# Hybrid decoder trunk on one core: in the last two feed-forward layers the high weights meet both activation parts in one 512-column product

## The chip, the cores and the metric

The kernel runs on one core of one Trainium2 chip. The metric is the device time of one execution in microseconds; of several runs the median counts. The engines are named as in the profile: PE is TensorE (PEld its weight loads), DVE is VectorE, ACT is ScalarE, POOL is GpSimd, SP issues most of the DMAs.

## The reference

The input is a sequence of 256 tokens with 1024 features, float32. Four residual layers follow one another; each applies a token mixer (attention, gated spatial unit, state-space layer, attention again) and then a channel mixer, the feed-forward block that the change is about:

```
def causal_depthwise_conv(h, w, b):
    hp = jnp.pad(h, ((0, 0), (CONV_K - 1, 0), (0, 0)))
    y = hp[:, 0:L] * w[0]
    for kk in range(1, CONV_K):
        y = y + hp[:, kk:kk + L] * w[kk]
    return y + b

def conv_gated_ffn(xn, w_up, conv_w, conv_b, w_down):
    h = causal_depthwise_conv(xn @ w_up, conv_w, conv_b)   # 1024 -> 2 * 2816
    a, g = jnp.split(h, 2, axis=-1)
    return (jax.nn.silu(g) * a) @ w_down                   # 2816 -> 1024

for i in range(4):
    x = x + mixer_i(rmsnorm(x, ...))
    x = x + conv_gated_ffn(rmsnorm(x, ...), ...)
return rmsnorm(x, final_norm_g)
```

## The kernel before, in words

**Split products.** Every matrix product keeps float32 precision by splitting both factors into a high part (rounded to the matmul's input format fp32r) and a low part (the rest). A product is then three matmuls into the same PSUM region: high weights by high activations, high weights by low activations, low weights by high activations. `mm_feat` (lines 119 to 126) does this with the weights as the stationary operand and the activations as the moving one: line 124 is wh by xth, line 125 is wh by xtl, line 126 is wl by xth, each with 256 columns, the 256 tokens. `mm_tok` (lines 128 to 134) does it the other way round, with 256 or 512 columns of weights as the moving operand. The activations lie in two tiles, `xth` and `xtl` of [128, 8, 256], made by `new_xt` and filled by `xt_evac`.

**Weights.** `Weights` streams tiles of 1 MB through three raw buffers. `half` turns half a tile into its high part on ACT (line 71) and its low part on DVE (line 72); there are six buffers for each part. Each iteration of a loop prepares one tile, four tiles ahead of use: two halves are called from `evac` (lines 414 and 418), the rest from `step`.

**Phases.** The plan runs eight phases one after the other: attention, feed-forward 0, gated unit, feed-forward 1, state-space layer (S5), feed-forward 2, attention, feed-forward 3. The program fixes the order of instructions on each engine; engines wait for one another by semaphores.

**The feed-forward phase.** There are 22 "up" units, u0 to u21. Each has two blocks of 128 output features: s=1, the gate, and s=0, the value. There are 11 "down" units, d0 to d10. `proj_feat` does one s of one up unit: 8 steps of k, each three matmuls, so 24 matmuls for an s and 48 for a unit. `down` does 24 matmuls of 512 columns. PSUM has eight banks of 512 float32: banks 0 to 3 hold the sums of the down products; u_m writes bank 4 + m%4, s=0 in the left half, s=1 in the right half. u0, u1 and u2 are done early, in the heads of the phase, token by token, and are transposed (line 368) into banks 4, 5 and 6 in the middle of u3, which itself writes bank 7. The order is then u4, u5, d0, u6, u7, d1, and so on to u16, u17, d6, then u18, u19, u20, u21, d7, and the tail d8, d9, d10, once for each half of the tokens.

**Evacuation.** `evac` of a unit stands in program order behind the matmuls of the next unit. For each s, ACT reads the bank and writes y = tap 2 times the value plus bias (line 406); then DVE adds the other two taps from the same bank, shifted by one and two tokens (line 410, two instructions for each s, so four a unit). Then come half a weight tile, silu on ACT (line 416), the gate product on DVE (line 417), another half a tile, and the split of the result into gh (ACT) and gl (DVE), lines 198 and 199. In the iteration of u3, `evac` handles u0, u1 and u2 together; u3's own `evac` comes in the iteration of u4. The loop also calls `w.step()` after each `evac`.

**S5** uses the space of the `xth` and `xtl` tiles for two tables, TT, once their last products are done (lines 1114 to 1121).

Of the kernel before, what the change touches and what calls it, by code (L numbers as in the profile page):

```python
# [8 lines left out]
F32 = mybir.dt.float32  # L9
F32R = mybir.dt.float32r  # L10
BF16 = mybir.dt.bfloat16
AF = mybir.ActivationFunctionType
ALU = mybir.AluOpType
# [84 lines left out]
class K:  # L98
# [65 lines left out]
        return r  # L164

    def new_xt(self):
        self.xth = self.big.tile([128, 8, 256], F32R, tag="xth", name="xth")
        self.xtl = self.big.tile([128, 8, 256], F32R, tag="xtl", name="xtl")

    def to_xt(self, b, xn, banks):  # L170
        for q in range(2):
# [38 lines left out]
    def proj_feat(self, n, p, s):  # L210

        for k in range(8):
            self.mm_feat(p[:, 256 * s:256 * s + 256], n, slice(256 * k + 128 * s, 256 * k + 128 * s + 128),
                         k, s == 0 and k == 0, s == 1 and k == 7)

    def proj_tok(self, n, b, p):

        t = slice(128 * b, 128 * b + 128)
        for k in range(8):
            self.mm_tok(p, self.xth[:, k, t], self.xtl[:, k, t], n, slice(256 * k, 256 * k + 256), k == 0, k == 7)  # L220
# [106 lines left out]
class FFN(Phase):  # L327
# [44 lines left out]
    def body(self):  # L372
        k, w = self.k, self.k.w
        pend = []
        for kind, a in self.order()[3:-3]:
            n = w.take()
            if kind == "u":
                p = k.bank(4 + a % 4)
                k.proj_feat(n, p, 0)
                if a == 3:  # L380
                    for m in range(3):
                        self.transposes(m, k.bank(4 + m))
                        pend.append((m, k.bank(4 + m)))
                k.proj_feat(n, p, 1)
                e = [(a, p)]
            else:
                k.down(self.gt[a], n, self.acc, (0, 1), a == 0, False)
                e = []
            self.evac(pend)
            pend = e  # L390
            w.step()
            for _ in range(1 + (kind == "d" and a % 2)):
                next(self.bg, None)
        self.evac(pend)
        for _ in self.bg:
            pass

    def evac(self, items):
        nc, cw = self.nc, self.cw
        ys = []  # L400
        for m, p in items:
            y = self.tmp.tile([128, 512], F32, tag="y", name="y")
            ys.append(y)
            for s in (1, 0):
                cs = slice(256 * s, 256 * s + 256)
                nc.scalar.activation(y[:, cs], p[:, cs], AF.Identity, scale=cw[:, s, m, 2:3], bias=cw[:, s, m, 3:4])  # L406
            for s in (1, 0):
                o = 256 * s
                for tap in (1, 2):
                    nc.vector.scalar_tensor_tensor(  # L410
                        y[:, o + tap:o + 256], p[:, o:o + 256 - tap], cw[:, s, m, 2 - tap:3 - tap],
                        y[:, o + tap:o + 256], ALU.mult, ALU.add)
        w = self.k.w
        w.half_to(w.use + w.ap)
        for (m, p), y in zip(items, ys):
            nc.scalar.activation(y[:, 256:512], y[:, 256:512], AF.Silu)  # L416
            nc.vector.tensor_tensor(out=y[:, 0:256], in0=y[:, 256:512], in1=y[:, 0:256], op=ALU.mult)  # L417
        w.half_to(w.use + w.ap)
        for (m, p), y in zip(items, ys):
            if m % 2 == 0:  # L420
                self.gt[m // 2] = self.k.new_gt()
            self.k.split(self.gt[m // 2], m % 2, y[:, 0:256])
# [313 lines left out]
class S5(Phase):  # L736
# [368 lines left out]
    def body(self):  # L1105
        k, nc, w = self.k, self.nc, self.k.w
        ut = k.pst[:, 4:8, :].rearrange("p b (a t) -> p (b a) t", a=2)
        n = w.take()
# [2 lines left out]
            FFN.transposes(self, m, k.bank(4 + m))  # L1111
        k.proj_feat(n, k.bank(7), 1)
        tabs = [w.take() for _ in range(5)]
        TT = []
        for i, tag in enumerate(("xth", "xtl")):
            t = k.big.tile([128, 2048], F32, tag=tag, name=f"T{i}")
            TT.append(t)

        for c in (slice(0, 512), slice(512, 1536)):
            for i in range(2):  # L1120
                nc.sync.dma_start(TT[i][:, c], self.d_t[i][:, c.start + 512:c.stop + 512])
        gt0, p0, bb, gt1, p1 = (w.hl[t] for t in tabs)
# [21 lines left out]
        def scan(i, mid=lambda: None):  # L1144
# [10 lines left out]
            sh = [128, 2, 8, 64]  # L1155
            T = [self.t0[:, 512 * r:512 * r + 512] if i == 0 else TT[r][:, 512 * (i - 1):512 * i] for r in range(2)]
            T = [v.rearrange("p (a c) -> p a c", a=8).unsqueeze(1).to_broadcast(sh) for v in T]
# [107 lines left out]
        n = w.take()  # L1265
# [113 lines left out]
```

## Time and profile before

| | |
|---|---|
| median of 3 runs | 1209.46 us (1208.31 to 1211.32) |
| the profiled execution, its own time | 1211.12 us |
| its span, first to last instruction | 1209.3 us |
| mean granted TensorE clock | 0.990 |
| matmuls, weight loads | 9072 each |
| DVE busy | 895.8 us (74%) |
| ACT busy | 707.3 us (58%) |

A row of the timeline gives the start in us, the length in us, engine, line, operation, output and inputs with shapes, and the count of merged instructions; a bracket at its end gives the idle time before it and what ended it. A row of instruction groups gives the count, then busy time in us and the mean of one in ns, then the idle time before the group. Matmuls are pipelined: the length printed for one overlaps with the next, so the pace of PE is read from the distance between starts. A row of the stages gives, for each engine, busy us and the number of instructions, and at the end the granted TensorE clock (1.00 is full), the DMA share and GB/s.

### The profile page before, as it was taken

How to read it: one execution, taken by the hardware profiler on the slowest of the kernel's cores; microseconds unless marked ns; L12 is line 12 of the kernel's file. 1: busy time of each engine (PE TensorE's matmuls, PEld its weight loads, DVE VectorE, ACT ScalarE, POOL GpSimd, SP SyncE). 2: the span in 40 equal slices, each digit the busy share in tenths (PEclk: the TensorE clock that was granted, in tenths of full speed). 3: DMA queues.
4: the chain of work that ended last, by engine and by line, in shares of the span. 5: the costliest groups of instructions: out<-in, count | busy, mean ns of one | idle time of the engine just before them, and what ended most of it. 6: DMA issues, size and time to landing. Idle time of an engine off the chain costs nothing.

```text
span 1209.3 us, 21995 instructions
## 1 busy us (share of the span) xinstructions
PE 1182.2 (98%) x9072; PEld 1083.6 (90%) x9072; DVE 895.8 (74%) x1268; ACT 707.3 (58%) x1076; POOL 166.3 (14%) x308
## 2 busy tenths in 40 slices
PE   8999999999999999999987999999999999999997
PEld 6898999999898999999976899999988989999996
DVE  5665689799767599899569769776766656886673
ACT  5665576557554574667474657565555655665551
POOL 3885000000286001000122000000000000000000
PEclk8999999999999999999998999999999999999999
DMA  7633368787656355777861645645535333564530
GB/s 295 224 105 122 144 220 283 232 296 258 233 209 209 114 218 220 228 268 263 316 251 68 224 180 194 243 161 202 193 120 225 109 123 112 207 242 175 209 123 35
DMA packets 49557, 237.46 MB, mean 196 GB/s; under 512 B 14896, under 2 KB 15792, under 8 KB 24240
## 3 DMA queue, kind: packets, MB, share of 16 engines
q1 hardware_dynamic: 46208, 223.73, 51.3%
q0 software_dynamic: 3104, 12.06, 2.5%
q8 instruction: 71, 1.16, 0.4%
q10 hardware_dynamic: 144, 0.26, 0.1%
q14 instruction: 30, 0.25, 0.1%
HBM read 222.79 MB, written 13.24 MB: 195 GB/s over the span
## 4 chain that ended last, share of the span: by engine, by line
PE 90%; DVE 5%; ACT 2%; DMA 1%; issue 1%; DVEq 0%; SPq 0%; POOLq 0%; POOL 0%; ACTq 0%
PE pst L124 15%; PE pst L126 15%; PE pst L125 15%; PE pst L132 13%; PE pst L134 13%; PE pst L133 13%; PE pst L536 1%; PE pst L179 1%; DVE wl L72 1%; PE pst L512 1%; DVE t L1166 1%; PE pst L553 1%; DVE wl L68 1%; DVE t L1169 1%; ACT wh L71 1%
## 5 line engine op out<-in xcount | busy, mean ns | idle before, releaser
L72 DVE TENSOR_TENSOR wl<-raw,wh 128x1024 fp32r<-128x1024 f32 x344 | 415.0, 1231 | 60.0 <-ACT wh L71 59.8
L124 PE MATMUL pst<-xth,wh 128*128 128x256 f32 x1552 | 441.0, 284 | 0.0
L125 PE MATMUL pst<-xtl,wh 128*128 128x256 f32 x1552 | 439.2, 283 | 0.0
L126 PE MATMUL pst<-xth,wl 128*128 128x256 f32 x1552 | 439.1, 283 | 0.0
L71 ACT ACTIVATE wh<-raw 128x1024 fp32r<-128x1024 f32 x344 | 350.3, 1048 | 9.4 <-DMA raw<-in_up_dram 4.3
L124 PEld LDWEIGHTS pst<-xth,wh 128*128 128x128 f32 x1552 | 297.7, 192 | 2.3
L125 PEld LDWEIGHTS pst<-xtl,wh 128*128 128x128 f32 x1552 | 297.8, 192 | 1.2
L126 PEld LDWEIGHTS pst<-xth,wl 128*128 128x128 f32 x1552 | 297.7, 192 | 0.0
L410 DVE SCALAR_TENSOR_TENSOR y<-pst,cw,y 128x255 f32<-128x255 f32 x352 | 160.7, 479 | 72.8 <-ACT y L406 66.6
L132 PE MATMUL pst<-wh,gh 128*128 128x512 f32 x512 | 202.7, 396 | 1.6 <-ACT gh L689 1.6
L133 PE MATMUL pst<-wl,gh 128*128 128x512 f32 x512 | 201.0, 393 | 0.0
L134 PE MATMUL pst<-wh,gl 128*128 128x512 f32 x512 | 200.8, 392 | 0.0
L406 ACT ACTIVATE y<-pst,cw 128x256 f32<-128x256 f32 x176 | 88.1, 557 | 69.4 <-PE pst L126 64.9
L132 PEld LDWEIGHTS pst<-wh,gh 128*128 128x128 f32 x512 | 97.1, 190 | 21.7 <-ACT gh L689 2.1
L134 PEld LDWEIGHTS pst<-wh,gl 128*128 128x128 f32 x512 | 96.8, 189 | 21.1 <-DVE gl L690 0.4
L133 PEld LDWEIGHTS pst<-wl,gh 128*128 128x128 f32 x512 | 97.0, 190 | 18.6
L132 PE MATMUL pst<-wh,xth 128*128 128x256 f32 (+1 forms) x336 | 105.9, 315 | 0.0
L134 PE MATMUL pst<-wh,xtl 128*128 128x256 f32 (+1 forms) x336 | 105.3, 313 | 0.0
L133 PE MATMUL pst<-wl,xth 128*128 128x256 f32 (+1 forms) x336 | 105.3, 313 | 0.0
L163 POOL TENSOR_TENSOR r<-m,mhalf 128x1 f32<-128x1 f32 x20 | 11.1, 554 | 684.7 <-DVE m L161 676.2
L416 ACT ACTIVATE y<-y 128x256 f32<-128x256 f32 x88 | 36.4, 419 | 75.3 <-DVE y L410 75.3
L198 ACT ACTIVATE gh<-y 128x256 fp32r<-128x256 f32 x88 | 36.1, 418 | 75.2 <-DVE y L417 75.2
(167 smaller groups left out, 1219.2 us busy)
## 6 DMA issues: line engine op xcount, KB each, us to landing
raw<-in_up_dram SPq DMA_DIRECT2D x88, 1024.0 KB, 5.0
raw<-in_down_dram SPq DMA_DIRECT2D x44, 1024.0 KB, 4.9
raw<-in_wqk_dram SPq DMA_DIRECT2D x16, 1024.0 KB, 4.9
raw<-in_wo_dram SPq DMA_DIRECT2D x8, 1024.0 KB, 4.8
raw<-in_glu_dram SPq DMA_DIRECT2D x8, 1024.0 KB, 5.9
raw<-in_wv_dram SPq DMA_DIRECT2D x7, 1024.0 KB, 5.2
gb<-in_g_dram SPq DMA_DIRECT2D x9, 512.0 KB, 5.7
d_gt<-gf POOLq DMA_DIRECT2D x4, 1024.0 KB, 7.7
```

The source lines that it names most:

```text
L71: nc.scalar.activation(h[:, s], r[:, s], AF.Copy)
L72: nc.vector.tensor_tensor(out=l[:, s], in0=r[:, s], in1=h[:, s], op=ALU.subtract)
L124: nc.tensor.matmul(out, h[:, cols], xh, start=first, stop=False, skip_group_check=True)
L125: nc.tensor.matmul(out, h[:, cols], xl, start=False, stop=False, skip_group_check=True)
L126: nc.tensor.matmul(out, l[:, cols], xh, start=False, stop=last, skip_group_check=True)
L132: nc.tensor.matmul(out, ah, h[:, cols], start=first, stop=False, skip_group_check=True)
L133: nc.tensor.matmul(out, ah, l[:, cols], start=False, stop=False, skip_group_check=True)
L134: nc.tensor.matmul(out, al, h[:, cols], start=False, stop=last, skip_group_check=True)
L198: self.nc.scalar.activation(g[0][:, j], src, AF.Copy)
L406: nc.scalar.activation(y[:, cs], p[:, cs], AF.Identity, scale=cw[:, s, m, 2:3], bias=cw[:, s, m, 3:4])
L410: nc.vector.scalar_tensor_tensor(y[:, o + tap:o + 256], p[:, o:o + 256 - tap], cw[:, s, m, 2 - tap:3 - tap], y[:, o + tap:o + 256], ALU.mu ...
L416: nc.scalar.activation(y[:, 256:512], y[:, 256:512], AF.Silu)
```

## The change

In feed-forward 2 and 3 (`self.i > 1`), the units u4 to u21 use a new function, `proj_wide`. The two activation parts lie side by side for each k in one tile `xt` of [128, 8, 2, 256]; the names `xth` and `xtl` become views of it, and S5's two tables become halves of one tile in its place. For each k, the high weights are loaded once and meet both parts in one matmul of 512 columns: the left half of the bank gets wh by xth, the right half wh by xtl. A second matmul of 256 columns adds wl by xth to the left half. A unit now fills two banks, s=0 one and s=1 the next: 4 and 5 for even units, 6 and 7 for odd ones. `evac` first copies both right halves to a tile z on ACT, then DVE adds the left halves to it in place; from there it goes on as before, but reads z (SBUF) where it read the bank (PSUM). The rest of the kernel is the same, u0 to u3 and feed-forward 0 and 1 included.

```
     def new_xt(self):
-        self.xth = self.big.tile([128, 8, 256], F32R, tag="xth", name="xth")
-        self.xtl = self.big.tile([128, 8, 256], F32R, tag="xtl", name="xtl")
+        self.xt = self.big.tile([128, 8, 2, 256], F32R, tag="xt", name="xt")
+        self.xth, self.xtl = self.xt[:, :, 0], self.xt[:, :, 1]
...
+    def proj_wide(self, n, p):
+        h, l = self.w.hl[n]
+        for s in range(2):
+            for k in range(8):
+                c = slice(256 * k + 128 * s, 256 * k + 128 * s + 128)
+                self.nc.tensor.matmul(p[:, s], h[:, c], self.xt[:, k].rearrange("p a t -> p (a t)"),
+                                      start=k == 0, stop=False, skip_group_check=True)
+                self.nc.tensor.matmul(p[:, s, 0:256], l[:, c], self.xth[:, k], start=False, stop=k == 7,
+                                      skip_group_check=True)
...
         for kind, a in self.order()[3:-3]:
             n = w.take()
-            if kind == "u":
+            if kind == "u" and a > 3 and self.i > 1:
+                p = k.pst[:, 4 + 2 * (a % 2):6 + 2 * (a % 2)]
+                k.proj_wide(n, p)
+                e = [(a, p)]
+            elif kind == "u":
                 p = k.bank(4 + a % 4)
...
         for m, p in items:
+            if len(p.shape) == 3:
+                z = self.tmp.tile([128, 2, 256], F32, tag="z", name="z")
+                nc.scalar.activation(z[:, :, :], p[:, :, 256:512], AF.Copy)
+                nc.vector.tensor_tensor(out=z[:, :, :], in0=p[:, :, 0:256], in1=z[:, :, :], op=ALU.add)
+                p = z[:, :, :].rearrange("p s t -> p (s t)")
             y = self.tmp.tile([128, 512], F32, tag="y", name="y")
...
-        TT = []
-        for i, tag in enumerate(("xth", "xtl")):
-            t = k.big.tile([128, 2048], F32, tag=tag, name=f"T{i}")
-            TT.append(t)
+        t = k.big.tile([128, 2, 2048], F32, tag="xt", name="T")
+        TT = [t[:, i] for i in range(2)]
```

## The prediction

> **What bounds the kernel now.** I read the profile's page first, then the chain of waits, the instruction groups, and the timeline of feed-forward 2. The page's first rows and the chain agree on the bound:
>
> ```profile
> PE 1182.2 (98%) x9072; PEld 1083.6 (90%) x9072; DVE 895.8 (74%) x1268; ACT 707.3 (58%) x1076; POOL 166.3 (14%) x308
> PE 90%; DVE 5%; ACT 2%; DMA 1%; issue 1%; DVEq 0%; SPq 0%; POOLq 0%; POOL 0%; ACTq 0%
> ```
>
> PE is the chain for 90% of the span. So an edit pays if it shortens PE's stream, and costs if it makes PE wait. How long a matmul really occupies PE stands in the distance between starts, here at the end of an up unit, at the down unit behind it, and at another down unit:
>
> ```profile
> 805.75 0.28 PE L124 MATMUL pst<-xth,wh 128*128 128x256 f32 x1
> 808.51 0.28 PE L126 MATMUL pst<-xth,wl 128*128 128x256 f32 x1
> 808.63 0.40 PE L132 MATMUL pst<-wh,gh 128*128 128x512 f32 x1
> 812.29 0.39 PE L133 MATMUL pst<-wl,gh 128*128 128x512 f32 x1
> 760.22 0.39 PE L134 MATMUL pst<-wh,gl 128*128 128x512 f32 x1
> 762.93 0.39 PE L134 MATMUL pst<-wh,gl 128*128 128x512 f32 x1
> 787.15 1.91 DVE L410 SCALAR_TENSOR_TENSOR y<-pst,cw,y 128x255 f32<-128x255 f32 x4 [4.05 <-ACT y L406]
> 804.13 1.91 DVE L410 SCALAR_TENSOR_TENSOR y<-pst,cw,y 128x255 f32<-128x255 f32 x4 [4.05 <-ACT y L406]
> ```
>
> From 805.75 to 808.51 there are 23 steps: 0.120 us for 256 columns. From 808.63 to 812.29 there are 16 steps of 512 columns, 0.2288 us each; from 760.22 to 762.93 there are 12, 0.2258 each. For whole units I use the period of one group (two up units, one down unit): the same evacuation recurs 16.98 us later; 96 matmuls at 0.120 are 11.52, which leaves 5.46 for 24 matmuls, 0.2275 each. Twice 256 columns cost 0.240 us, once 512 costs 0.2275. Something of about 13 ns is paid per matmul.
>
> **The change, part by part.** *The wide product.* Each step of k and s had three narrow matmuls, 0.360 us. It now has one wide and one narrow, 0.2275 + 0.120 = 0.3475: 12.5 ns less (11.2 to 14.2 by the two other rows). Units u4 to u21 have 18 x 16 = 288 such steps a layer, so 3.6 us a layer, 7.2 in both, if PE never waits. The count of columns through the array is the same; only 576 matmuls with their weight loads are gone.
>
> *The banks.* A unit now takes two banks, and u5's s=1 takes bank 7. Before, u5 had bank 5 and bank 7 was next written by u7. Bank 7 holds u3, which is evacuated the old way, behind the evacuations of u0, u1 and u2. This is how DVE and PE stood at that place:
>
> ```profile
> 726.75 5.54 DVE L410 SCALAR_TENSOR_TENSOR y<-pst,cw,y 128x255 f32<-128x255 f32 x12 [0.70 <-ACT y L406]
> 732.21 1.21 DVE L72 TENSOR_TENSOR wl<-raw,wh 128x1024 fp32r<-128x1024 f32 x1
> 733.34 1.08 DVE L417 TENSOR_TENSOR y<-y 128x256 f32<-128x256 f32 x3
> 734.35 1.22 DVE L72 TENSOR_TENSOR wl<-raw,wh 128x1024 fp32r<-128x1024 f32 x1
> 735.48 1.09 DVE L199 TENSOR_TENSOR gl<-y,gh 128x256 fp32r<-128x256 f32 x3
> 736.49 2.35 DVE L72 TENSOR_TENSOR wl<-raw,wh 128x1024 fp32r<-128x1024 f32 x2
> 738.76 1.90 DVE L410 SCALAR_TENSOR_TENSOR y<-pst,cw,y 128x255 f32<-128x255 f32 x4
> 743.52 1.91 DVE L410 SCALAR_TENSOR_TENSOR y<-pst,cw,y 128x255 f32<-128x255 f32 x4
> 726.68 0.28 PE L124 MATMUL pst<-xth,wh 128*128 128x256 f32 x1
> 737.83 0.28 PE L124 MATMUL pst<-xth,wh 128*128 128x256 f32 x1
> 1046.83 0.28 PE L124 MATMUL pst<-xth,wh 128*128 128x256 f32 x1
> 1047.76 1.90 DVE L410 SCALAR_TENSOR_TENSOR y<-pst,cw,y 128x255 f32<-128x255 f32 x4
> ```
>
> DVE has no gap here from 726.75 on. The row at 738.76 is u3's four taps; they end at 738.76 + 1.90 = 740.66, and only then is bank 7 free. On PE, 726.68 is the second step of u3's s=1. Seven steps of 0.36 end u3 at 729.20, the 16 of u4 lead to 734.96 and eight of u5's s=0 to 737.83, where u5's s=1 began. With wide products PE gets there 24 x 0.0125 = 0.3 us earlier, at 737.53. Nothing on DVE or ACT ahead of 740.66 is changed, so PE stands until DVE is done. How soon PE follows the engine it waits for:
>
> ```profile
> 384.96 0.64 ACT gh L689
> 385.64 0.50 PE L132 MATMUL pst<-wh,gh 128*128 128x512 f32 x1 [1.63 <-ACT gh L689]
> 386.36 0.70 PE L134 MATMUL pst<-wh,gl 128*128 128x512 f32 x1
> 390.12 0.40 PE L134 MATMUL pst<-wh,gl 128*128 128x512 f32 x1
> 384.00:385.00 1.00, 0.00 (x1) 0.00 (x0) 0.89 (x2) 0.04 (x1) 0.00 (x0) 1.00 0.91 320
> 387.00:388.00 1.00, 1.00 (x4) 0.81 (x3) 1.00 (x2) 0.48 (x1) 0.00 (x0) 0.50 0.96 352
> 390.00:391.00 1.00, 1.00 (x6) 0.81 (x5) 0.45 (x1) 0.29 (x2) 0.00 (x0) 1.00 0.54 123
> ```
>
> ACT ended at 385.60, PE started at 385.64: 0.04 us. So u5's s=1 starts at 740.70 and not at 737.83: 2.87 us late, after a wait of 740.70 - 737.53 = 3.17 us. In feed-forward 3 the taps end at 1049.66 and the old start was 1046.83: 2.87 again. Queued behind the waiting matmul on PE is all that follows: the rest of u5, d0, u6. On the other side u4's s=1 needs bank 5 some 2.8 us after 729.20; the second third of the 12 taps, u1's, ends 3.7 us after 726.75, at 730.4. It does not wait. u5's s=0 needs bank 6 at 734.7, free at 732.3.
>
> Behind that point 264 steps are left in the layer (8 of u5, 16 units of 16): 264 x 0.0125 = 3.30 us are won back (2.96 to 3.75). What was won ahead of it is swallowed by the wait.
>
> *The clock.* The rows above show what a stop of PE does besides. PE stood for 1.63 us by the bracket (the row of 384 to 385 has nothing of PE busy) and from 386.36 ran at half clock (0.50 in the row of 387 to 388) until about 390. From 386.36 to 390.12 there are 9 steps of 512 columns in 3.76 us, where 9 x 0.2275 is 2.05: 1.71 us lost. The new wait is longer, so I expect the same drop in both layers. There it came 2.35 us after PE stopped (386.36 less 384.01); in a wait of 3.17 some 0.8 us of the slow stretch could fall into the wait itself, which lowers the loss to 1.71 x 2.94 / 3.76 = 1.3. I take 1.6 (1.3 to 1.7).
>
> *Copy and sum.* The work that evacuation gains, by its nearest rows:
>
> ```profile
> L406 ACT ACTIVATE y<-pst,cw 128x256 f32<-128x256 f32 x176 | 88.1, 557 | 69.4 <-PE pst L126 64.9
> L198 ACT ACTIVATE gh<-y 128x256 fp32r<-128x256 f32 x88 | 36.1, 418 | 75.2 <-DVE y L417 75.2
> L185 ACT ACTIVATE xth<-pst 128x512 fp32r<-128x512 f32 x32 | 17.7, 596 | 35.8 <-PE pst L179 35.7
> L190 DVE TENSOR_TENSOR x<-pst,x 128x512 f32<-128x512 f32 x28 | 19.1, 688 | 23.7 <-PE pst L134 23.7
> 809.89 1.91 DVE L410 SCALAR_TENSOR_TENSOR y<-pst,cw,y 128x255 f32<-128x255 f32 x4 [0.91 <-ACT y L406]
> 872.35 1.91 DVE L410 SCALAR_TENSOR_TENSOR y<-pst,cw,y 128x255 f32<-128x255 f32 x4 [0.91 <-ACT y L406]
> 877.17 2.36 DVE L72 TENSOR_TENSOR wl<-raw,wh 128x1024 fp32r<-128x1024 f32 x2
> 883.56 0.69 DVE L190 TENSOR_TENSOR x<-pst,x 128x512 f32<-128x512 f32 x1 [4.03 <-PE pst L134]
> ```
>
> ACT copies 512 elements from PSUM in 0.60 us (L185), DVE adds 512 in 0.69 (L190). y then comes from SBUF, 0.42 instead of 0.56 (L198 for L406). The taps can begin 0.60 + 0.69 + 0.42 - 0.56 = 1.15 us later. In a group DVE idles 4.05 + 0.91 = 4.96 us ahead of its two evacuations; the group gets 0.4 us shorter and the two evacuations 2.3 longer, so 2.2 us of idle are left. Weights are prepared four tiles ahead, over 16 us of PE. This costs nothing as long as that idle lasts. u18 to u21 have no down unit between them: there only 0.91 is free for each against 1.15 + 0.2, and DVE falls back by 4 x 0.44 = 1.8 us. Behind u21, gl was done at 877.17, and d10 needed it: the first sum over d10 came at 883.56, behind its first 6 matmuls, so d10 began near 882.2. Of 5.0 us, 1.8 + 1.15 are used; about 2 remain. Banks come free earlier than before, with the add.
>
> *One tile for both parts, and T in its place.* The same engines read and write the same elements in the same order; the two old tiles were released by matmuls standing next to each other. Nothing, at most one matmul (0.12 us) either way.
>
> *The sum.* Per layer 2.87 + 1.6 - 3.30 = +1.2 us (0.8 to 3.2 for both layers from the bounds), together +2.3. The profiled execution took 1211.12 us for a span of 1209.3, so it would be 1213.4; against the median of 1209.46, 1.7 below that execution, it is 1211.8. That is 0.2% slower, inside the 0.3% (3.6 us) that a measurement of this kernel can tell from no change.
>
> **The rivals.** *No wait at bank 7*, if PE does not in fact reach it ahead of DVE: then the full 7.2 us come in, 1202.3. Against it stands DVE's row without a gap to 740.66; u3 would have to be evacuated over 3 us earlier. 8%.
>
> *The wait without the clock drop*: 2 x (2.87 - 3.30) = -0.9 us, 1208.6. The Trainium skill speaks for it: "TensorE: Matmul & The Clock Gate", section "What's actually happening", lets the clock fall to half only after an idle window of about 3.4 us, longer than this wait. The trace does not agree: 1.63 us idle were followed by a clock of 0.50. 14%.
>
> *The wide product saves nothing*, because a 512-column matmul with activations as the moving operand takes as long as two narrow ones. Then the late start and the slow clock stay and nothing is won back: 2 x (2.87 + 1.6) = +8.9 us, 1218.4. This is the slower case; it goes over +3.6 us once a step saves less than (4.47 - 1.8) / 264 = 10 ns. For it: no row of before streams 512 columns of activations. Against it:
>
> ```profile
> L132 PE MATMUL pst<-wh,xth 128*128 128x256 f32 x240 | 68.3, 284 | 0.0
> L124 PE MATMUL pst<-xth,wh 128*128 128x256 f32 x1552 | 441.0, 284 | 0.0
> ```
>
> At 256 columns it makes no difference which of the two streams, 284 ns each. The same page of the Trainium skill, section "Back-to-back issue gap", points the same way as this rival: columns / 2.4 + 2.5 ns make a pair only 2.5 ns dearer than one wide product; by it, as an estimate, the sum would be about +7.6 us. The trace has 12.5. 6%.
>
> *DVE becomes the bound* in u18 to u21 or the tail, if copy and sum cost twice what I took. That is beyond any row here: 2%.
>
> **How the numbers follow.** The forecast has 70%: 1210.3 to 1212.7 by its bounds, and medians scatter by about 1.5 us. With the case without a clock drop (1208.6, or 1207.7 with the larger saving) the range is 1206 to 1215. Left out are the other cases and some tails. Faster by over 0.3% (below 1205.8): the first rival and a little, 0.10. Slower (above 1213.1): the last two, 8%, and the upper end of the forecast, 12%: 0.20. Within: 0.70.
>
> **What would show it.** Right: in both layers one gap of PE of about 3.2 us in the middle of u5, ended by DVE's taps of u3; behind it a granted clock of 0.5 for over 3 us; wide and narrow starts 0.2275 and 0.120 apart; no other gap on PE. Wrong: no gap there, a second gap at u20 or d10, or a step of 0.36.

## The result, and the profile after

The changed kernel is slower: 1216.61 us median of 6 runs (1215.24 to 1220.81) against 1209.94 (1208.31 to 1211.46) for the kernel before, a ratio of 1.0058 with a 95% interval of 1.0041 to 1.0076. The profiled execution took 1216.67 us, its span is 1214.9 us, 5.6 us more than before. The forecast was 1211.8 with a range of 1206 to 1215.

The page shows the removed matmuls, and that the chain is still PE's: 576 matmuls fewer, and yet hardly less busy time.

```profile
PE 1180.1 (97%) x8496; PEld 1053.7 (87%) x8496; DVE 919.5 (76%) x1304; ACT 725.7 (60%) x1112; POOL 166.1 (14%) x308
PE 89%; DVE 6%; ACT 2%; issue 1%; DMA 1%; DVEq 0%; SPq 0%; POOLq 0%; ACTq 0%
```

In the changed kernel's numbering, line 223 is the wide product, 225 the narrow one, 420 the copy to z, 421 the sum, 427 the tap with the bias, 431 the two other taps. The waits of PE from feed-forward 2 to the end are these (line, releaser: us in all, times, longest):

```profile
PE pst L223 <- DVE y L431: 5.9, 2, 3.0
PE pst L557 <- DVE sl L548: 0.5, 1, 0.5
```

The second stood in the kernel before as well. The first is new: one wait of 3 us in each of the two layers, ended by DVE's taps. Here is the place in feed-forward 2: on DVE the twelve taps of u0 to u2 and u3's four, then on PE the last narrow product ahead of the wait, the first wide product of u5's second half, and the first matmul of the down unit behind it:

```profile
726.48 5.54 DVE L431 SCALAR_TENSOR_TENSOR y<-pst,cw,y 128x255 f32<-128x255 f32 x12 [0.70 <-ACT y L427]
738.49 1.90 DVE L431 SCALAR_TENSOR_TENSOR y<-pst,cw,y 128x255 f32<-128x255 f32 x4
737.29 0.28 PE L225 MATMUL pst<-xt,wl 128*128 128x256 f32 x1
740.54 0.47 PE L223 MATMUL pst<-xt,wh 128*128 128x512 f32 x1 [2.97 <-DVE y L431]
744.89 0.47 PE L132 MATMUL pst<-wh,gh 128*128 128x512 f32 x1
```

The granted clock is the number third from the right in these rows of the stages:

```profile
738.00:739.00 1.00, 0.00 (x0) 0.00 (x0) 0.96 (x2) 0.35 (x1) 0.00 (x0) 1.00 1.03 434
743.00:744.00 1.00, 1.00 (x4) 0.84 (x4) 0.93 (x2) 0.03 (x1) 0.00 (x0) 0.50 0.16 25
```

The taps end at 740.39, PE goes on at 740.54. The eight steps of that half take from 740.54 to 744.89, 4.35 us, at a granted clock of 0.50 in the row of 743 to 744.

The pace of the products, in an undisturbed unit and the down unit behind it:

```profile
806.44 0.40 PE L223 MATMUL pst<-xt,wh 128*128 128x512 f32 x1
806.67 0.28 PE L225 MATMUL pst<-xt,wl 128*128 128x256 f32 x1
811.74 0.40 PE L223 MATMUL pst<-xt,wh 128*128 128x512 f32 x1
811.97 0.28 PE L225 MATMUL pst<-xt,wl 128*128 128x256 f32 x1
812.09 0.40 PE L132 MATMUL pst<-wh,gh 128*128 128x512 f32 x1
817.59 0.39 PE L223 MATMUL pst<-xt,wh 128*128 128x512 f32 x1
```

From 806.44 to 812.09 there are 16 steps of a wide and a narrow product: 0.353 us each. It was 0.360 with three narrow ones; the prediction had 0.3475. A step saves 7.0 ns instead of 12.5.

With these sizes the prediction's own sum comes out. The start at bank 7 stands 740.54 + 0.27 - 737.83 = 2.98 us late (DVE's row of twelve taps, here at 726.48, stood at 726.75 before, so 0.27 puts the two traces on one scale). The slow clock costs 4.35 - 8 x 0.353 = 1.53 us. Won back are 264 x 7.0 ns = 1.85 us. That makes 2.7 us a layer and 5.3 for both; the spans differ by 5.6, and 5.9 from this place on, where the changed kernel is 0.27 ahead. Most of the rest lies in the down units, which the prediction took as unchanged. Behind an alternating unit one takes 5.50 us (812.09 to 817.59 above); before, it took 5.47, from 808.63 to the first matmul of the next up unit:

```profile
814.10 0.28 PE L124 MATMUL pst<-xth,wh 128*128 128x256 f32 x1
```

There are fourteen such down units in the two layers, which makes 0.4 to 0.5 us.

### The profile page after: what moved, and what is told of

Same layout as the page of the kernel before. It is cut to its first block, busy times and chain, and to the rows that moved or that the text cites. A ratio compares the mean times of both kernels' runs of the same rounds, so it can differ in the third digit from the quotient of the medians.

```text
span 1214.9 us, 20913 instructions
## 1 busy us (share of the span) xinstructions
PE 1180.1 (97%) x8496; PEld 1053.7 (87%) x8496; DVE 919.5 (76%) x1304; ACT 725.7 (60%) x1112; POOL 166.1 (14%) x308
## 4 chain that ended last, share of the span: by engine, by line
PE 89%; DVE 6%; ACT 2%; issue 1%; DMA 1%; DVEq 0%; SPq 0%; POOLq 0%; ACTq 0%
PE pst L132 13%; PE pst L134 13%; PE pst L133 13%; PE pst L223 10%; PE pst L124 9%; PE pst L125 9%; PE pst L126 9%; PE pst L225 5%; PE pst L557 1%; PE pst L179 1%; DVE wl L72 1%; PE pst L533 1%; DVE t L1185 1%; PE pst L574 1%; DVE y L431 1%
## 5 line engine op out<-in xcount | busy, mean ns | idle before, releaser
L124 PE MATMUL pst<-xt,wh 128*128 128x256 f32 x976 | 278.1, 285 | 0.0
L125 PE MATMUL pst<-xt,wh 128*128 128x256 f32 x976 | 276.1, 283 | 0.0
L126 PE MATMUL pst<-xt,wl 128*128 128x256 f32 x976 | 276.1, 283 | 0.0
L223 PE MATMUL pst<-xt,wh 128*128 128x512 f32 x576 | 207.0, 403 | 5.9 <-DVE y L431 5.9
L124 PEld LDWEIGHTS pst<-xt,wh 128*128 128x128 f32 x976 | 187.2, 192 | 1.7
L125 PEld LDWEIGHTS pst<-xt,wh 128*128 128x128 f32 x976 | 187.2, 192 | 0.7
L126 PEld LDWEIGHTS pst<-xt,wl 128*128 128x128 f32 x976 | 187.2, 192 | 0.0
L225 PE MATMUL pst<-xt,wl 128*128 128x256 f32 x576 | 163.0, 283 | 0.0
L223 PEld LDWEIGHTS pst<-xt,wh 128*128 128x128 f32 x576 | 109.6, 190 | 33.6 <-ACT y L437 6.5
L225 PEld LDWEIGHTS pst<-xt,wl 128*128 128x128 f32 x576 | 110.2, 191 | 0.5
L132 PE MATMUL pst<-wh,xt 128*128 128x256 f32 (+1 forms) x336 | 105.9, 315 | 0.0
L134 PE MATMUL pst<-wh,xt 128*128 128x256 f32 (+1 forms) x336 | 105.3, 313 | 0.0
L133 PE MATMUL pst<-wl,xt 128*128 128x256 f32 (+1 forms) x336 | 105.2, 313 | 0.0
```

The costliest lines, as they stand in the source:

```text
L124: nc.tensor.matmul(out, h[:, cols], xh, start=first, stop=False, skip_group_check=True)
L125: nc.tensor.matmul(out, h[:, cols], xl, start=False, stop=False, skip_group_check=True)
L126: nc.tensor.matmul(out, l[:, cols], xh, start=False, stop=last, skip_group_check=True)
L132: nc.tensor.matmul(out, ah, h[:, cols], start=first, stop=False, skip_group_check=True)
L133: nc.tensor.matmul(out, ah, l[:, cols], start=False, stop=False, skip_group_check=True)
L134: nc.tensor.matmul(out, al, h[:, cols], start=False, stop=last, skip_group_check=True)
```

## Experiments

The question left by the two traces: are the wait and the slow clock the whole loss, and why does a step save only 7 ns? The theory was that wait, clock and step make up the whole of it, and that copy, sum and tile layout cost nothing. The rivals were that the longer evacuation slows the layers everywhere, and, for the step, that 512 columns of activations are slow in themselves rather than in alternation with 256. The kernel before ran beside each group of experiments, at 1210.0 to 1210.9 us; ratios are to it.

**Wide from u6 on.**

```
-            if kind == "u" and a > 3 and self.i > 1:
+            if kind == "u" and a > 5 and self.i > 1:
```

> The wide product starts at u6 instead of u4; u4 and u5 go the old way into banks 4 and 5. Theory: the loss is the wait of u5 at bank 7 with the half clock behind it, 2.9 + 1.6 us in each of the two layers, and a wide step saves only 6.7 ns (0.3533 for 0.360). Then both gaps and the slow stretches go, 256 steps a layer save 1.7 us, and the time is before less 3.4: about 1206.5. Rival: copy and sum in the evacuation, or the new tile layout, slow the layers everywhere; then the time stays above before, about 1211 to 1214, though the gaps are gone.

Measured: 1210.3 us, ratio 0.9994 (0.9985 to 1.0003). The loss is gone, but the kernel is only 0.7 us below before by the ratio, where the theory gave 3.4. The trace shows why: a shorter wait has taken the old one's place.

```profile
746.32 1.91 DVE L431 SCALAR_TENSOR_TENSOR y<-pst,cw,y 128x255 f32<-128x255 f32 x4
748.38 0.47 PE L223 MATMUL pst<-xt,wh 128*128 128x512 f32 x1 [1.21 <-DVE y L431]
```

The stage behind it:

```profile
750.00:751.00 1.00, 1.00 (x8) 0.87 (x7) 1.00 (x2) 1.00 (x2) 0.00 (x0) 1.00 0.22 90
```

u6's second half goes to bank 5, and u5, which now lies there, is evacuated until 748.23. The wait is 1.21 us a layer, and behind it the clock stays at 1.00. So the expectation failed on the same point as the edit under study: which bank is read last. The rival is not settled by this run.

**Wide and narrow products in groups of eight**, in the changed kernel.

```
-            for k in range(8):
-                wide(k); narrow(k)
+            for k in range(8):
+                wide(k)
+            for k in range(8):
+                narrow(k)
```

> The changed kernel, but for each s first the eight wide products, then the eight narrow ones, the same sums in another order. Theory A: the lost 6 ns of a step come from the turn between 512 and 256 columns; eight wide and eight narrow then take 8 x 0.2275 + 8 x 0.120, a step is near 0.348 and the time about 3 us below the changed kernel, 1213.6. Theory B: a product with 512 columns of activations takes 0.235 wherever it stands; then a step stays at 0.353 and the time at 1216.6.

Measured: 1212.93 us, ratio 1.0024 (1.0014 to 1.0034), 3.7 us below the changed kernel. The order of the same matmuls is worth that much. Theory B gives nothing for it and falls; theory A's reason, a price for each turn, is tested by the pairs below. The two waits at bank 7 are still there:

```profile
PE pst L224 <- DVE y L433: 6.2, 2, 3.1
```

**Both edits together.**

> Both edits: wide from u6 on, and wide and narrow products in groups of eight. Theory A (the turns cost): before less 2 x 256 x 12.5 ns = 6.4 us, about 1203.5. Theory B (the 512 columns cost): like the start at u6 alone, about 1206.5.

Measured: 1208.28 us, ratio 0.9979 (0.9969 to 0.9989). Neither number was met. The wait at bank 5 is here as well, 2.5 us in the two layers, and takes them off the 5.6 that 2 x 256 steps of 0.349 would save:

```profile
PE pst L224 <- DVE y L433: 2.5, 2, 1.3
```

**Two banks, copy and sum, but three narrow products.**

```
-                matmul(p[:, s], h[:, c], xt[:, k] as 512 columns, start=k == 0, ...)
+                matmul(p[:, s, 0:256], h[:, c], self.xth[:, k], start=k == 0, ...)
+                matmul(p[:, s, 256:512], h[:, c], self.xtl[:, k], start=False, ...)
```

> The changed kernel with its two banks, its copy and its sum, but three narrow products: high weights by the low part go to the right half by themselves. A step costs 0.360 again. Theory: the wait at bank 7 and the half clock are all there is of loss, so before plus 2 x (2.9 + 1.6) = 9 us, about 1219, and 3 to 3.5 us above the changed kernel. Rival: the step of 0.353 comes from copy and sum beside it and not from the wide product; then the narrow steps are slowed as well, to 0.366 or so, and the time is about 1222.

Measured: 1219.26 us, ratio 1.0065 (1.0052 to 1.0077), so +7.9 us by the ratio, where 9 were expected. Copy and sum do not slow the narrow steps: from 785.34 in its timeline to 796.14, line 223, the first of a step's three, recurs every 0.36.

```profile
785.34 0.28 PE L223 MATMUL pst<-xt,wh 128*128 128x256 f32 x1
796.14 0.28 PE L223 MATMUL pst<-xt,wh 128*128 128x256 f32 x1
```

30 steps in 10.80 us are 0.360 each. The waits at bank 7 are nearly as long as in the changed kernel (2.8 us for 3.0):

```profile
PE pst L223 <- DVE y L433: 5.6, 2, 2.8
```

This kernel has the change's banks and evacuation without its gain, and loses what the waits and the slow clock make.

**Groups of eight from u6 on, banks exchanged**, so that u6 takes 6 and 7 and u7 takes 4 and 5.

```
-                p = k.pst[:, 4 + 2 * (a % 2):6 + 2 * (a % 2)]
+                p = k.pst[:, 6 - 2 * (a % 2):8 - 2 * (a % 2)]
```

> Wide from u6 on, wide and narrow products in groups of eight, and the pairs of banks exchanged: even units take 6 and 7, odd ones 4 and 5. u6 then writes bank 7, whose reader u3 is long done, and u7's second half goes to bank 5, more than 5 us after u6's second half would have. Theory: the 1.25 us that PE still waited at u6 with the start at u6 go in both layers, no gap is left, and a step at 0.349 saves 256 x 11.2 ns a layer: before less 5.7 us, 2.5 below the version without the exchange, about 1205. Rival: the wait moves on to u7 (bank 5) or u8; then the time stays near 1208.

Measured: 1204.8 us, ratio 0.9952 (0.9938 to 0.9966): 5.8 us below before by the ratio, 5.7 expected. PE has no wait left in the two layers' up units; the waits from feed-forward 2 on are

```profile
PE pst L559 <- DVE sl L550: 0.5, 1, 0.5
PE pst L179 <- DVE xn L155: 0.3, 1, 0.3
```

Copy, sum and the common tile are all in this kernel, and it runs where the steps alone put it. The rival that they cost time everywhere falls. The steps, wide and narrow in turn of eight:

```profile
784.98 2.00 PE L224 MATMUL pst<-xt,wh 128*128 128x512 f32 x8
786.82 1.12 PE L227 MATMUL pst<-xt,wl 128*128 128x256 f32 x8
787.77 2.00 PE L224 MATMUL pst<-xt,wh 128*128 128x512 f32 x8
790.57 0.40 PE L132 MATMUL pst<-wh,gh 128*128 128x512 f32 x1
```

784.98 to 790.57 are 16 steps of 0.349.

**The wait filled with matmuls**, in the changed kernel, ahead of u5's second half.

```
+            for _ in range(12 if s and fill else 0):       # fill: only for u5
+                matmul(self.bank(0), h[:, 0:128], xt[:, 0] as 512 columns, start=True, stop=True)
```

> The changed kernel with twelve wide products more in the middle of u5, into bank 0, which the down products overwrite later; they fill most of the 3 us in which PE waits for bank 7. The wait itself stays as long. Theory: half the loss at that place is the half clock after the wait; with PE kept busy the clock stays at 1.00 and some 1.5 us a layer come back: about 3 us below the changed kernel. Rival: the clock falls for another reason or costs nothing on the path; then the time stays that of the changed kernel or is longer.

Measured: 1213.78 us, ratio 1.0026 (1.0017 to 1.0035), 2.8 us below the changed kernel by the medians and 3.9 by the ratios. The wait is as long; only what PE does in it differs, and the clock stays up:

```profile
737.39 2.91 PE L222 MATMUL pst<-xt,wh 128*128 128x512 f32 x12
740.52 0.47 PE L226 MATMUL pst<-xt,wh 128*128 128x512 f32 x1 [0.23 <-DVE y L434]
```

The stage behind it:

```profile
741.00:745.00 4.00, 4.00 (x23) 3.40 (x23) 3.33 (x6) 1.95 (x5) 0.00 (x0) 1.00 0.66 233
```

So the slow clock is worth 1.4 us a layer on the path by the medians and 1.9 by the ratios, and it comes from PE's standing still.

**Groups of sixteen**, banks exchanged.

> As the exchange of banks with groups, but all sixteen wide products of a unit first and then all sixteen narrow ones. Theory A: a wide product is slow only shortly after narrow ones; fewer turns bring a step from 0.349 to about 0.3475, so up to 1 us less than with groups of eight. Theory B: 0.230 is the steady time of a wide product here; then the same time as with groups of eight.

Measured: 1204.5 us, ratio 0.9953 (0.994 to 0.9965), like groups of eight.

```profile
785.26 3.82 PE L223 MATMUL pst<-xt,wh 128*128 128x512 f32 x16
788.92 2.08 PE L228 MATMUL pst<-xt,wl 128*128 128x256 f32 x16
790.83 0.40 PE L132 MATMUL pst<-wh,gh 128*128 128x512 f32 x1
```

Sixteen wide ones take 3.66 us, 0.2288 each; sixteen narrow ones 1.91, 0.1194 each; a step 0.348. It can't be told by the time from 0.349.

**Wide products alone**: the product of low weights and high activations is left out in u6 to u21 of both layers.

> u6 to u21 of the two layers leave out the narrow product of low weights and high activations; only wide products are left, sixteen in a row. Theory A (only the turn costs): after the first few they stand 0.2267 us apart, as in the down units. Theory B (512 columns of activations are slow in themselves): 0.235. The whole time falls by less than 2 x 256 x 0.12 = 61 us, since VectorE then sets the pace: about 1165.

Measured: one run, 1179.31 us. The starts in one unit:

```profile
776.03 0.63 PE L223 MATMUL pst<-xt,wh 128*128 128x512 f32 x2
779.02 0.62 PE L223 MATMUL pst<-xt,wh 128*128 128x512 f32 x2
```

There are 13 steps between them, 0.230 each. But these stand right behind a wait; the sixteen of the next unit, behind a down unit, go from 784.91 to 788.31:

```profile
784.91 0.39 PE L223 MATMUL pst<-xt,wh 128*128 128x512 f32 x1
788.31 0.39 PE L223 MATMUL pst<-xt,wh 128*128 128x512 f32 x1
```

That is 15 steps of 0.2267, theory A's number and the pace of the down units. 512 columns of activations in a row are not the slow case. The time fell by some 30 us where about 45 were expected, since PE now waits for DVE's sums:

```profile
PE pst L223 <- DVE z L419: 25.4, 13, 4.6
```

With units this short, DVE holds PE up.

**In turn, without the wait**: from u6 on, banks exchanged, wide and narrow alternating as in the change.

> Wide from u6 on with the exchanged banks, but wide and narrow products in turn as in the change: the wide product alone, without wait and without slow clock. Theory: a step stays at 0.353, 256 steps a layer save 7.0 ns each, so before less 3.6 us, 2 us above the groups of eight. Rival: without the wait the turns run at 0.347, as they did right behind a wait; then it is as fast as the groups, before less 6.

Measured: 1207.53 us, ratio 0.9977 (0.9967 to 0.9987), -2.8 us by the ratio, -3.6 expected. In its timeline the 32 steps of two units go from 780.32 to 791.61, 0.353 each, so the rival falls. The change's product by itself is a gain, a small one.

**In pairs**: two wide, then two narrow.

> The same with two wide, then two narrow products. Theory A: each turn has its price; half the turns leave half the loss, a step of 0.350 to 0.351, before less 4.6 to 5.1 us. Theory B: only strict alternation loses; then a step of 0.347 to 0.349 and before less 5.7 or more, as with groups of eight.

Measured: 1204.69 us, ratio 0.9953 (0.994 to 0.9967), -5.7 us.

```profile
784.69 0.63 PE L223 MATMUL pst<-xt,wh 128*128 128x512 f32 x2
790.03 0.39 PE L227 MATMUL pst<-xt,wl 128*128 128x256 f32 x2
790.26 0.40 PE L132 MATMUL pst<-wh,gh 128*128 128x512 f32 x1
```

16 steps from 784.69 to 790.26 are 0.348 each. Pairs are as good as sixteens. So it isn't a price per turn, which would have left half the loss; only strict alternation loses, about 5 ns a step (theory B).

## Why the prediction was wrong

**The wait at bank 7** was right in place and size: 3.17 us forecast, 2.97 measured in both layers, start 2.98 us late for 2.87. The hand-over took 0.15 us, not 0.04. Nothing else in the up units waits, as forecast.

**The clock** came out right: 1.6 us forecast, 1.53 in the trace, 1.4 to 1.9 by the run with the wait filled. But there was luck in it. The stop of 1.63 us that the term was taken from stands in every trace, 1.63 to 1.64 us long, and only in the trace of before did the clock fall behind it. In the other eleven it stayed at 1.00, here in the changed kernel:

```profile
386.23 0.50 PE L132 MATMUL pst<-wh,gh 128*128 128x512 f32 x1 [1.64 <-ACT gh L710]
387.00:388.00 1.00, 1.00 (x5) 0.82 (x6) 0.84 (x1) 1.00 (x2) 0.00 (x0) 1.00 0.93 385
```

Behind the waits at bank 7 it fell each time: two of 2.97 us in the changed kernel, two of 3.08 with groups of eight, two of 2.82 with three narrow products. Behind the waits of 1.21 to 1.26 us at bank 5 it never did. So the rival without a drop fell, for which "TensorE: Matmul & The Clock Gate" of the Trainium skill spoke (section "What's actually happening", an idle window of about 3.4 us). With that section eleven of the twelve stops of 1.63 to 1.64 us agree, and none of the six waits at bank 7, which are shorter than that window. How long a stop must be for the clock to fall surely, no run shows.

**The step is what failed**: "it now has one wide and one narrow, 0.2275 + 0.120 = 0.3475: 12.5 ns less (11.2 to 14.2 by the two other rows)". It measured 0.353, 7.0 ns less. The pace of a uniform run was taken for that of two kinds in alternation, and so were the bounds, which all came from uniform runs. In pairs and longer groups the forecast's number holds (0.348); in strict turns it does not. With 264 steps in each of the two layers that is 2 x 264 x 5.5 ns = 2.9 us, which takes the forecast of +2.3 to +5.2. With the slower down units, which the prediction left at nothing, it is 5.6 to 5.7, and the spans differ by 5.6. The medians differ by 6.7, and the ratio's interval, 5.0 to 9.2 us, holds both.

**The rival "the wide product saves nothing"** had put the turning point at 10 ns a step. The 7.0 measured lie below it, and so the result fell on the slower side, past the 0.3%, though the product does save something. Its reason, slow activations, was not the cause: alone, they pace at 0.2267. By the formula that the same page of the Trainium skill gives in its section "Back-to-back issue gap" for an isolated matmul, one wide product for two narrow ones would save 2.5 ns. The runs show 12 in groups and 7 in turns, so for this kernel's stream of products that formula is too low in either order.

**Copy and sum** cost nothing on the path, as forecast. The rows behind that:

```profile
L427 ACT ACTIVATE y<-z,cw 128x256 f32<-128x256 f32 x72 | 39.4, 595 | 38.1 <-DVE z L421 38.1
L421 DVE TENSOR_TENSOR z<-pst,z 128x512 f32<-128x512 f32 x36 | 24.7, 686 | 23.4 <-ACT z L420 23.4
L420 ACT ACTIVATE z<-pst 128x512 f32<-128x512 f32 x36 | 21.1, 586 | 33.2 <-PE pst L225 33.2
807.27 0.69 DVE L421 TENSOR_TENSOR z<-pst,z 128x512 f32<-128x512 f32 x1 [2.11 <-ACT z L420]
```

The copy takes 0.59 and the sum 0.69, as taken. Making y from SBUF was to take 0.42 and takes 0.595: the row that was used is a plain copy, while this instruction takes scale and bias from a tile. From PSUM it took 0.557 in the kernel before, so the move to SBUF gained nothing, and the taps begin some 1.3 us later instead of 1.15. DVE still idles 2.11 us ahead of the first sum of a group, so this too stays off the path.

**What stays open**: why strict alternation is 5 ns a step slower. It isn't ACT or DVE beside it, since the steps are as long where both are idle. In the changed kernel they are from 788.4 to 789.8, by the stage's row (third and fourth pair), and by the timeline the wide products start there at 788.24, 788.59, 788.93 and 789.30: three steps in 1.06 us, 0.353 each, as elsewhere:

```profile
788.40:789.80 1.40, 1.40 (x9) 1.21 (x9) 0.00 (x0) 0.00 (x0) 0.00 (x0) 1.00 1.03 439
```

The loss is not spread evenly. To the nanosecond of the trace, the steps there take 349, 350 and 361 ns, over and over.

Nor is it fixed to the two shapes. In the run with wide products from u6 on, the steps behind its wait alternated at full clock, and did so at 0.347 to the end of the next unit, u7:

```profile
748.80 0.40 PE L223 MATMUL pst<-xt,wh 128*128 128x512 f32 x1
755.39 0.39 PE L223 MATMUL pst<-xt,wh 128*128 128x512 f32 x1
```

19 steps, 0.347 each. In the run with the wait filled, six steps from 740.95 to 743.03 were 0.347 each too, behind twelve wide products and a stop of only 0.23 us. In both runs the pace was 0.353 again behind the next down unit. What lies behind that was not settled.

## What to carry to other kernels

When a unit of work takes more buffers, look at the first use of each buffer under the new numbering and ask who read it last: here one bank, twice, cost more than 528 cheaper steps could win, and starting two units later, exchanging two pairs of banks and putting the products in pairs or longer groups turned the change into a gain of 0.5%. Take the pace of an instruction from a run with the same neighbours; the pace of uniform runs was only the best case for the mix here, and a mix is worth trying in pairs. A wait of PE near 3 us cost half as much again here, because the clock fell behind it. And look for the same event in a second trace before taking a price from one.

## What the runs showed of the hardware

Alternating matmuls of 512 and 256 columns took 0.353 us a pair; the same matmuls two and two, eight and eight or sixteen and sixteen took 0.348 to 0.349; behind a stop of PE, of 1.21 us in one run and 0.23 us in another, alternation ran at 0.347 until the next down unit. Stops of 1.21 to 1.26 us left the granted clock at 1.00, and six of 2.82 to 3.08 us were each followed by a granted clock of 0.50, in the changed kernel for over 3 us. The same stop of 1.63 to 1.64 us was followed by 0.50 in one of twelve traces and by 1.00 in eleven.
